# Attention in a fused trunk kernel: one score round for each query tile over three PSUM banks, the product with V placed a step later

## The chip, the cores and the metric

The kernel runs on one core of one Trainium2 chip. The metric is the device time of one execution in microseconds (us). Engines are named as in the profile: PE is TensorE, DVE is VectorE, ACT is ScalarE, POOL is GpSimd, SP issues most transfers.

## What is computed

One layer of a hybrid trunk, for a prompt of 1024 tokens and 8 sample groups of 16 tokens (1152 tokens in all, D = 1024). One input projection feeds an attention branch and a Mamba-2 branch; both are projected back, gated, merged and added to x. All of it is float32. The part that the change touches is the attention of the prompt: 16 heads of 64, chunks of 64 tokens, each chunk attends to itself and to the eight chunks before it.

```python
def attend(q, k, v, bias, mask):
    s = jnp.einsum('bqhd,bkhd->bhqk', q, k).astype(jnp.float32) * (ATT_HEAD_DIM ** -0.5) + bias[None].astype(jnp.float32)
    s = jnp.where(mask, s, -1e30)
    p = jax.nn.softmax(s, axis=-1).astype(v.dtype)
    return jnp.einsum('bhqk,bkhd->bqhd', p, v)
```

## The kernel before

**Stages.** Norm and modulation come first, then the eight units of the attention (two heads each), then dt and the 16 head pairs of the second branch, then the projections. Every stage has a `dense_gen` with the large matmuls and generators with everything else. `run` (line 732) records the program: it draws dense matmuls one after the other, adds their cost to a planned `clock`, and lets the other generators (`urgent`, `paced`) take a step whenever the planned time and their credit allow. `until(t)` and `pause(t)` hold a generator until that planned time.

**Large matmuls.** A projection weight is split into a high and a low float32r part (ACT copy at line 321, DVE subtraction at line 322), the activations too, and each product is three matmuls of 128x128 by 384 columns: lines 384, 385 and 387 (`dense`) and 438 to 440 (`dense_tok`, for q, k and v of a unit, nine token tiles of 128). They accumulate in the two banks of pool `psd`.

**A unit's attention** runs beside the dense matmuls of the next unit. `prelude` normalises q and k on POOL, transposes them (lines 857 and 867) and splits them. `prompt` (line 915) then works on query tiles m = 0 to 7 of 128 tokens; tile m sees n = min(m, 4) + 1 key tiles, so four of the eight tiles see five, 640 columns. `sample` (line 979) does the sample tokens, with matmuls of 32-column tiles (lines 1002, 1005, 1028).

For a query tile, `prompt` does this:

- scores (line 939): six matmuls for each column range, three terms for each of two heads. The head's 64 dims are the rows, so the two heads use the two row halves of the array (64x128 tiles). The result goes to the one tile of pool `pss`, two banks, one for each head. With 640 columns there are two rounds of 320, the second behind the emptying of the first
- `negated` (line 901): DVE adds the bias and takes the smallest value, one instruction for each head and round
- `exps` (lines 896 to 898): ACT's exponential with the row sum, DVE's reciprocal and scaling, into places `S` of the arena
- a step later, `transposed` (lines 903 to 913): PE transposes the probabilities of tile m-1 in groups of up to four (line 908) through a bank `g` of pool `psg` (four banks); ACT (line 910) or DVE (line 912) copies them to another place `S`
- right behind, after a planned pause, the product with V of the same tile m-1 (line 969): 2n matmuls with 64 columns each, the two heads in the two column halves (128x64 tiles), into a bank `g`; DVE multiplies with the gate z (line 974).

**What sets the order.** The recorded program is reordered for each engine by a scheduler that uses durations of its own; engines then run their queues in order, with semaphores for every dependency. `late` (line 268) pins an instruction behind what was recorded before it on its engine; later recorded work can still be moved ahead of it. In the kernel before, the scores' and V's matmuls at lines 939 and 969 are not pinned, `negated` is. `sfree` is the planned time at which the score tile is free again; `walloc` waits for a place in the arena.

Of the kernel before, what the change touches and what calls it, by code (L numbers as in the profile page):

```python
# [18 lines left out]
NT = NP + NB * NS  # L19
G3 = NT // 3  # L20
NH = 16
HD = 64
# [89 lines left out]
def trunk_kernel(ctx: ExitStack, tc: tile.TileContext, h):  # L112
    nc = tc.nc
# [3 lines left out]
    pss = ctx.enter_context(tc.tile_pool(name="pss", bufs=1, space=bass.MemoryType.PSUM))  # L117
# [3 lines left out]
    arena = Arena(base, FCOLS)  # L121
# [46 lines left out]
    for n, w in PARAMS:  # L168
# [24 lines left out]
    Z0 = fixed[0] + 2 * 1024  # L193
    XW = 3 * 288 + 2 * 256
    L_RAW = arena.set_layout(fixed[0], [("raw", 2, 1024)])
    L_ATT = arena.set_layout(Z0, [("Q", 1, 18 * P), ("T", 5, NT), ("S", 8, 640), ("U", 2, 640), ("K", 4, 512), ("q", 2, 256), ("d", 2, 256),
                                  ("p", 2, 128), ("n", 2, 36 + 3 * 16), ("t", 4, 14)])
    L_ATT["Z"] = L_ATT["T"][2:]
    L_SSD = arena.set_layout(Z0, [("X", 1, XW), ("R", 2, 1184), ("t", 8, 36), ("pad", 1, 576), ("T", 9, NT), ("Y", 1, 1184), ("H", 1, 1024),
# [68 lines left out]
    late = tc.keep_in_program_order  # L268
# [61 lines left out]
    def get_w(i):  # L330
        while w_left(i):
            w_split(i)
        return wsplit[i][:2]
# [119 lines left out]
    for k in range(KT):  # L453
        b = alloc(L_START, "T", NT)
# [73 lines left out]
    ms = {}  # L528
# [73 lines left out]
    v = [sm.ap[:, i * 9:(i + 1) * 9] for i in range(4)]  # L602
# [15 lines left out]
    x = xs_in[0]  # L618
# [13 lines left out]
    for g, tok in enumerate(groups):  # L632
        ps = pg(G3)
# [43 lines left out]
    get_w(2)  # L677
    z_first = alloc(L_ATT, "T", NT)
    d_first = alloc(L_ATT, "T", NT)

# [15 lines left out]
    clock = [0.0]  # L696
# [91 lines left out]
    sfree = [0.0]  # L788
    zs = {0: z_first}

    def attention(u):
        st = {"n": 0}
        lay = L_ATT
        big = "Z" if u == NU - 1 else "T"
# [99 lines left out]
        def exps(p, sm_, e):  # L894

            nc.scalar.activation(p, p, AF.Exp, bias=sm_[:, 4 + e:5 + e], scale=-1.0, accum_out=sm_[:, 6 + e:7 + e])  # L896
            nc.vector.reciprocal(sm_[:, 8 + e:9 + e], sm_[:, 6 + e:7 + e])
            nc.vector.tensor_scalar(p, p, sm_[:, 8 + e:9 + e], None, ALU.mult)

        def negated(p, least, ps, bap):  # L900
            late(nc.vector.tensor_tensor_reduce(p, ps, bap, -1.0, 3.0e38, ALU.add, ALU.min, least))  # L901

        def transposed(p, pt, nt):
            for j in range(0, nt, 4):
                n = min(4, nt - j)
                ps = pg()
                for s in range(n):
                    nc.tensor.transpose(ps[:, s * P:(s + 1) * P], p.ap[:, (j + s) * P:(j + s + 1) * P], ident)  # L908
                if j == 0:
                    nc.scalar.activation(pt.ap[:, j * P:(j + n) * P], ps[:, :n * P], AF.Copy)  # L910
                else:
                    nc.vector.tensor_copy(pt.ap[:, j * P:(j + n) * P], ps[:, :n * P])
            p.free()

        def prompt():
            yield from ready(lambda: "left" in st)
            yield from until(st["t"])
            qh, ql, kh, kl = st["ops"]
            v, z, bias = (st[n] for n in ("v", "z", "bias"))
            prev = None  # L920
            for m in range(9):
                n = min(m, 4) + 1
                np_ = min(m - 1, 4) + 1
                pr, pts = [], []
                if m < 8:

                    for e in range(2):
                        pr.append([(yield from walloc(lay, "S", 640)), 0])
                    sm_ = yield from walloc(lay, "t", 14)
                    cols = [(0, 320), (320, 320)] if n == 5 else [(0, n * P)]  # L930
                    qs = slice(m * P, m * P + P)
                    for a, (c, w) in enumerate(cols):
                        yield from until(sfree[0])
                        ps = pss.tile([P, 2, 512], F32, tag="s", name=nm("s"))
                        kk = slice((m + 1 - n) * P + c, (m + 1 - n) * P + c + w)
                        for i, (x, y) in enumerate(((qh, kh), (qh, kl), (ql, kh))):
                            for e in range(2):
                                hs = slice(HD * e, HD * e + HD)
                                nc.tensor.matmul(ps[:, e, :w], x.r[hs, qs], y.r[hs, kk], start=i == 0, stop=i == 2)  # L939
                        for e in range(2):  # L940
                            b = bias[e].ap[:, (5 - n) * P + c:(5 - n) * P + c + w]
                            least = sm_.ap[:, 2 * a + e:2 * a + e + 1] if n == 5 else sm_.ap[:, 4 + e:5 + e]
                            negated(pr[e][0].ap[:, c:c + w], least, ps[:, e, :w], b)
                        yield 3 * (w / 2.27 + 10)
                        sfree[0] = clock[0] + 2 * (w + 160) + 300
                    if n == 5:
                        nc.vector.tensor_tensor(sm_.ap[:, 4:6], sm_.ap[:, 0:2], sm_.ap[:, 2:4], ALU.min)
                    for e in range(2):
                        exps(pr[e][0].ap[:, :n * P], sm_.ap, e)
                        pr[e][1] = clock[0] + 3800 + 700 * e  # L950
                    sm_.free()
                if m == 7:
                    for x in st["ops"]:
                        x.free()
                    for b in bias:
                        b.free()
                if m:
                    for e in range(2):
                        pt = yield from walloc(lay, "S", 640)
                        yield from until(prev[e][1])  # L960
                        transposed(prev[e][0], pt, np_)
                        pts.append(pt)
                        yield 109 * np_
                    yield from pause(1100)
                    ps = pg(P)
                    for j in range(np_):
                        for e in range(2):
                            vc = (m - np_ + j) * P + e * HD
                            nc.tensor.matmul(ps[e * HD:e * HD + HD, :], v.ap[:, vc:vc + HD], pts[e].ap[:, j * P:(j + 1) * P],  # L969
                                             start=j == 0, stop=j == np_ - 1)  # L970
                    for x in pts:
                        x.free()
                    ms = slice((m - 1) * P, m * P)
                    nc.vector.scalar_tensor_tensor(z.ap[:, ms], ps, 0.5, z.ap[:, ms], ALU.mult, ALU.mult)
                    yield 2 * np_ * 103 + 200
                prev = pr
            done()

        def sample():
# [769 lines left out]
```

## Time and profile before

| what | value |
|---|---|
| median of 3 runs | 2037.41 us (2037.35 to 2038.08) |
| the profiled execution | 2043.03 us |
| its span, first to last instruction | 2041.2 us |
| instructions in it | 35394 |
| mean granted TensorE clock | 0.994 |
| chain of work that ended last | PE 96%, DVE 2%, DMA 1%, ACT 1% |
| scores of 320 columns, line 939 | 45.0 us (256) and 19.9 us (128, from `qa_att`) |
| product with V, line 969 | 84.3 us, 960 (two passes of each of 480) |
| transposes of probabilities, line 908 | 82.5 us, 560 |
| `negated`, line 901, DVE | 99.5 us, 208 |
| exponentials, line 896, ACT | 101.2 us, 144 |

The busy time of a group is the time that its instructions cover; matmuls overlap, so PE's groups are read by the starts of their instructions. A row of the timeline is start, duration, engine, line, form (rows*columns of the array's tile, and the moving operand) and how many were merged. A row of the stretches gives, behind the stretch and its length, the busy time of PE, weight loads (PEld), DVE, ACT and POOL, then the granted clock, the DMA share and GB/s.

### The profile page before, as it was taken

Reading aid. Unit: us, or ns where it says so; the run is one execution under the profiler, and the core shown is the slowest. Engines: PE = TensorE matmul, PEld = TensorE weight load, DVE = VectorE, ACT = ScalarE, POOL = GpSimd, SP = SyncE. Lnnn points to the kernel's source line nnn. Section 1 sums busy time; section 2 is a strip of 40 time slices with the busy share of each in tenths; the row PEclk is TensorE's granted clock in tenths of the full one; section 3 lists DMA queues with packets and bytes.
Section 4 is the critical chain, followed back from the end, with each engine's and each line's share of the span. In section 5 each row is a group of like instructions: output and inputs, shape, how many; then the busy total and the mean of one; then the engine's idle time right before and its main releaser. Section 6 shows DMA issues by size and latency. Waiting matters only on the chain.

```text
span 2041.2 us, 35394 instructions
## 1 busy us (share of the span) xinstructions
PE 2014.5 (99%) x14223; PEld 1879.7 (92%) x14223; DVE 1163.9 (57%) x2424; ACT 766.0 (38%) x1560; POOL 405.9 (20%) x657
## 2 busy tenths in 40 slices
PE   7999999999999999999999999999999999999999
PEld 5888888888888888999999999999999999999999
DVE  6445454554554566456775677557764533777732
ACT  5344443443434444444534444345443311111210
POOL 0123121231212210123332234224323210000000
PEclk9999999999999999999999999999998999999999
DMA  7233232332323232333333433243325663331331
GB/s 311 88 103 104 72 127 76 127 101 95 110 86 127 68 102 84 103 123 120 121 99 111 124 109 121 93 126 128 120 89 191 251 224 103 126 100 54 100 118 62
DMA packets 81371, 239.63 MB, mean 117 GB/s; under 512 B 14316, under 2 KB 15352, under 8 KB 81208
## 3 DMA queue, kind: packets, MB, share of 16 engines
q1 hardware_dynamic: 72248, 208.73, 31.3%
q0 software_dynamic: 8960, 28.65, 3.6%
q8 instruction: 112, 1.84, 0.4%
q14 instruction: 51, 0.42, 0.1%
HBM read 193.39 MB, written 43.95 MB: 116 GB/s over the span
## 4 chain that ended last, share of the span: by engine, by line
PE 96%; DVE 2%; DMA 1%; ACT 1%; issue 0%; SPq 0%; DVEq 0%; ACTq 0%
PE d L384 13%; PE d L387 13%; PE d L385 13%; PE s L384 5%; PE d L440 5%; PE s L385 5%; PE d L438 5%; PE s L387 5%; PE d L439 5%; PE g L969 4%; PE g L908 3%; PE s L939 3%; PE g L1385 2%; PE g L1358 1%; PE g L1405 1%; PE g L1028 1%
## 5 line engine op out<-in xcount | busy, mean ns | idle before, releaser
L384 PE MATMUL d<-rarena 128*128 128x384 f32 x1536 | 527.8, 344 | 1.0 <-ACT rarena L321 1.0
L385 PE MATMUL d<-rarena 128*128 128x384 f32 x1536 | 518.3, 337 | 0.0
L387 PE MATMUL d<-rarena 128*128 128x384 f32 x1536 | 517.5, 337 | 0.2 <-DVE rarena L322 0.2
L384 PEld LDWEIGHTS d<-rarena 128*128 128x128 f32 x1536 | 289.7, 189 | 6.3 <-issue 3.8
L387 PEld LDWEIGHTS d<-rarena 128*128 128x128 f32 x1536 | 289.4, 188 | 3.0 <-issue 2.1
L385 PEld LDWEIGHTS d<-rarena 128*128 128x128 f32 x1536 | 290.0, 189 | 1.8 <-issue 1.5
L321 ACT ACTIVATE rarena<-arena 128x1024 fp32r<-128x1024 f32 x97 | 102.6, 1058 | 301.0 <-PE s L385 188.6
L384 PE MATMUL s<-rarena 128*128 128x384 f32 x624 | 213.6, 342 | 1.3 <-DVE arena L901 1.3
L385 PE MATMUL s<-rarena 128*128 128x384 f32 x624 | 209.7, 336 | 0.0
L387 PE MATMUL s<-rarena 128*128 128x384 f32 x624 | 209.5, 336 | 0.0
L438 PE MATMUL d<-va_att,rarena 128*128 128x384 f32 x576 | 200.1, 347 | 0.3 <-DVE arena L689 0.3
L440 PE MATMUL d<-va_att,rarena 128*128 128x384 f32 x576 | 199.4, 346 | 0.0
L439 PE MATMUL d<-va_att,rarena 128*128 128x384 f32 x576 | 198.0, 344 | 0.0
L322 DVE TENSOR_TENSOR rarena<-arena,rarena 128x1024 fp32r<-128x1024 f32 x97 | 125.9, 1298 | 94.3 <-ACT rarena L321 93.3
L901 DVE CUSTOM_DVE_ANT_0 arena<-s,arena 128x320 f32<-128x320 f32 (+5 forms) x208 | 99.5, 513 | 135.1 <-PE s L939 112.3
L896 ACT ACTIVATE arena<-arena 128x640 f32<-128x640 f32 (+3 forms) x144 | 101.2, 706 | 97.0 <-DVE arena L901 51.8
L384 PEld LDWEIGHTS s<-rarena 128*128 128x128 f32 x624 | 117.8, 189 | 3.4 <-issue 1.6
L385 PEld LDWEIGHTS s<-rarena 128*128 128x128 f32 x624 | 117.9, 189 | 0.4 <-issue 0.4
L387 PEld LDWEIGHTS s<-rarena 128*128 128x128 f32 x624 | 117.6, 188 | 0.0
L440 PEld LDWEIGHTS d<-va_att,rarena 128*128 128x128 f32 x576 | 108.3, 188 | 7.0 <-issue 6.3
L438 PEld LDWEIGHTS d<-va_att,rarena 128*128 128x128 f32 x576 | 108.4, 188 | 6.8 <-issue 5.6
L910 ACT ACTIVATE arena<-g 128x512 f32<-128x512 f32 (+3 forms) x144 | 71.0, 522 | 114.0 <-PE g L908 113.6
(332 smaller groups left out, 3358.7 us busy)
## 6 DMA issues: line engine op xcount, KB each, us to landing
arena<-in_wall_dram SPq DMA_DIRECT2D x88, 512.0 KB, 3.9
arena<-in_kc_dram SPq DMA_DIRECT2D x64, 256.0 KB, 3.0
arena<-in_vc_dram SPq DMA_DIRECT2D x64, 256.0 KB, 2.8
arena<-acs_d SPq DMA_DIRECT2D x20, 576.0 KB, 3.6
gate_d<-arena POOLq DMA_DIRECT2D x48, 192.0 KB, 2.2
y_d<-arena POOLq DMA_DIRECT2D x15, 576.0 KB, 3.4
arena<-y_d SPq DMA_DIRECT2D x15, 576.0 KB
arena<-in_wssd_dram SPq DMA_DIRECT2D x16, 512.0 KB, 3.5
```

The costliest lines, as they stand in the source:

```text
L321: keep(nc.scalar.activation(hi.r[:, c], b.ap, AF.Copy))
L322: keep(nc.vector.tensor_tensor(lo.r[:, c], b.ap, hi.ap[:, c], ALU.subtract))
L384: nc.tensor.matmul(ps, hi.r[:, wc], kh.r[:, tok], start=k == 0, stop=False)
L385: nc.tensor.matmul(ps, hi.r[:, wc], kl.r[:, tok], start=False, stop=False)
L387: nc.tensor.matmul(ps, lo.r[:, wc], kh.r[:, tok], start=False, stop=k == nk - 1)
L438: nc.tensor.matmul(ps, kh.r[:, tok], hi.r[:, wc], start=k == 0, stop=False)
L439: nc.tensor.matmul(ps, kh.r[:, tok], lo.r[:, wc], start=False, stop=False)
L440: nc.tensor.matmul(ps, kl.r[:, tok], hi.r[:, wc], start=False, stop=k == KT - 1)
L896: nc.scalar.activation(p, p, AF.Exp, bias=sm_[:, 4 + e:5 + e], scale=-1.0, accum_out=sm_[:, 6 + e:7 + e])
L901: late(nc.vector.tensor_tensor_reduce(p, ps, bap, -1.0, 3.0e38, ALU.add, ALU.min, least))
L910: nc.scalar.activation(pt.ap[:, j * P:(j + n) * P], ps[:, :n * P], AF.Copy)
L969: nc.tensor.matmul(ps[e * HD:e * HD + HD, :], v.ap[:, vc:vc + HD], pts[e].ap[:, j * P:(j + 1) * P], start=j == 0, stop=j == np_ - 1)
```

## The change

The edit is in the arena's layout and in `prompt`. A tile of five key tiles gets its scores in one round: columns 0 to 319 go to the two banks of `pss`, columns 320 to 639 to two banks `g`, and the four `negated` follow together. The product with V is moved from tile m-1 to tile m-2, its matmuls are recorded directly behind the scores of tile m, and both are pinned with `late`; the loop has two more steps than tiles instead of one. The gate follows the round's `negated`. The planned times (`sfree`, `tpt`) change with it. The arena has nine places `S` instead of eight and one place `q` (squares of q and k, line 806) instead of two.

```diff
-    L_ATT = arena.set_layout(Z0, [("Q", 1, 18 * P), ("T", 5, NT), ("S", 8, 640), ("U", 2, 640), ("K", 4, 512), ("q", 2, 256), ("d", 2, 256),
+    L_ATT = arena.set_layout(Z0, [("Q", 1, 18 * P), ("T", 5, NT), ("S", 9, 640), ("U", 2, 640), ("K", 4, 512), ("q", 1, 256), ("d", 2, 256),
...
+            def weigh(j, po):
+                n = min(j, 4) + 1
+                for i in range(n):
+                    for e in range(2):
+                        vc = (j + 1 - n + i) * P + e * HD
+                        late(nc.tensor.matmul(po[e * HD:e * HD + HD, :], v.ap[:, vc:vc + HD], pts[j][e].ap[:, i * P:(i + 1) * P],
+                                              start=i == 0, stop=i == n - 1))
+                for x in pts.pop(j):
+                    x.free()
+                return 2 * n * 103 + 200
...
-            for m in range(9):
+            for m in range(10):
...
-                    cols = [(0, 320), (320, 320)] if n == 5 else [(0, n * P)]
-                    for a, (c, w) in enumerate(cols):
-                        yield from until(sfree[0])
-                        ps = pss.tile([P, 2, 512], F32, tag="s", name=nm("s"))
+                    yield from until(max(sfree[0], tpt.get(m - 2, 0.0)))
+                    ps = pss.tile([P, 2, 512], F32, tag="s", name=nm("s"))
+                    if m > 1:
+                        po = pg(P)
+                    cols = [(0, min(n * P, 512), [ps[:, e, :] for e in range(2)])]
+                    if n == 5:
+                        cols = [(0, 320, cols[0][2]), (320, 320, [pg() for _ in range(2)])]
...
-                                nc.tensor.matmul(ps[:, e, :w], x.r[hs, qs], y.r[hs, kk], start=i == 0, stop=i == 2)
+                                late(nc.tensor.matmul(pt[e][:, :w], x.r[hs, qs], y.r[hs, kk], start=i == 0, stop=i == 2))
+                        cost += 3 * (w / 2.27 + 10)
+                    if m > 1:
+                        cost += weigh(m - 2, po)
+                    for a, (c, w, pt) in enumerate(cols):
                         for e in range(2):
...
-                            negated(pr[e][0].ap[:, c:c + w], least, ps[:, e, :w], b)
-                        yield 3 * (w / 2.27 + 10)
-                        sfree[0] = clock[0] + 2 * (w + 160) + 300
+                            negated(pr[e].ap[:, c:c + w], least, pt[e][:, :w], b)
+                    yield cost
+                    sfree[0] = clock[0] + 2 * (n * P + 160) + 300
...
+                else:
+                    yield from until(tpt[m - 2])
+                    po = pg(P)
+                    yield weigh(m - 2, po)
+                if po is not None:
+                    gated(m - 2, po)
...
-                    yield from pause(1100)
-                    ps = pg(P)
-                    for j in range(np_):
-                        for e in range(2):
-                            vc = (m - np_ + j) * P + e * HD
-                            nc.tensor.matmul(ps[e * HD:e * HD + HD, :], v.ap[:, vc:vc + HD], pts[e].ap[:, j * P:(j + 1) * P],
-                                             start=j == 0, stop=j == np_ - 1)
-                    for x in pts:
-                        x.free()
-                    ms = slice((m - 1) * P, m * P)
-                    nc.vector.scalar_tensor_tensor(z.ap[:, ms], ps, 0.5, z.ap[:, ms], ALU.mult, ALU.mult)
-                    yield 2 * np_ * 103 + 200
-                prev = pr
+                    tpt[m - 1] = clock[0] + 1100
+                    sfree[0] = max(sfree[0], clock[0] + 1500)
```

More of the change, by code (lines that the diff above doesn't have):

```diff
@@ L919, in prompt, with gated @@
             v, z, bias = (st[n] for n in ("v", "z", "bias"))
-            prev = None
-            for m in range(9):
+            probs, pts, tpt = {}, {}, {}
+            def weigh(j, po):
[8 more added lines that the diff above has]
+                return 2 * n * 103 + 200
+            def gated(j, po):
+                ms = slice(j * P, (j + 1) * P)
+                nc.vector.scalar_tensor_tensor(z.ap[:, ms], po, 0.5, z.ap[:, ms], ALU.mult, ALU.mult)
+            for m in range(10):
                 n = min(m, 4) + 1
-                np_ = min(m - 1, 4) + 1
-                pr, pts = [], []
+                po = None
                 if m < 8:
+                    pr = []
                     for e in range(2):
-                        pr.append([(yield from walloc(lay, "S", 640)), 0])
+                        pr.append((yield from walloc(lay, "S", 640)))
                     sm_ = yield from walloc(lay, "t", 14)
-                    cols = [(0, 320), (320, 320)] if n == 5 else [(0, n * P)]
+                    yield from until(max(sfree[0], tpt.get(m - 2, 0.0)))
[5 more added lines that the diff above has]
+                        cols = [(0, 320, cols[0][2]), (320, 320, [pg() for _ in range(2)])]
                     qs = slice(m * P, m * P + P)
-                    for a, (c, w) in enumerate(cols):
-                        yield from until(sfree[0])
-                        ps = pss.tile([P, 2, 512], F32, tag="s", name=nm("s"))
+                    cost = 0
+                    for c, w, pt in cols:
                         kk = slice((m + 1 - n) * P + c, (m + 1 - n) * P + c + w)
@@ L948, in prompt @@
                     for e in range(2):
-                        exps(pr[e][0].ap[:, :n * P], sm_.ap, e)
-                        pr[e][1] = clock[0] + 3800 + 700 * e
+                        exps(pr[e].ap[:, :n * P], sm_.ap, e)
+                    probs[m] = pr, clock[0] + 3800
                     sm_.free()
+                else:
[4 more added lines that the diff above has]
+                    gated(m - 2, po)
                 if m == 7:
@@ L956, in prompt @@
                         b.free()
-                if m:
+                if 0 < m < 9:
+                    n = min(m - 1, 4) + 1
+                    pts[m - 1] = []
+                    pr, t0 = probs.pop(m - 1)
+                    yield from until(sfree[0])
                     for e in range(2):
                         pt = yield from walloc(lay, "S", 640)
[L960 to L963, printed above, removed]
-                    yield from pause(1100)
-                    ps = pg(P)
-                    for j in range(np_):
-                        for e in range(2):
-                            vc = (m - np_ + j) * P + e * HD
-                            nc.tensor.matmul(ps[e * HD:e * HD + HD, :], v.ap[:, vc:vc + HD], pts[e].ap[:, j * P:(j + 1) * P],
-                                             start=j == 0, stop=j == np_ - 1)
-                    for x in pts:
-                        x.free()
-                    ms = slice((m - 1) * P, m * P)
-                    nc.vector.scalar_tensor_tensor(z.ap[:, ms], ps, 0.5, z.ap[:, ms], ALU.mult, ALU.mult)
-                    yield 2 * np_ * 103 + 200
-                prev = pr
+                        yield from until(t0 + 700 * e)
+                        transposed(pr[e], pt, n)
+                        pts[m - 1].append(pt)
+                        yield 109 * n
+                    tpt[m - 1] = clock[0] + 1100
+                    sfree[0] = max(sfree[0], clock[0] + 1500)
             done()
```

## The prediction

> **What bounds the kernel now.** I read the engine line first, then a table by stretches, PE's waits, and the timeline of PE at the attention's own matmuls.
>
> ```profile
> PE 2014.5 (99%) x14223; PEld 1879.7 (92%) x14223; DVE 1163.9 (57%) x2424; ACT 766.0 (38%) x1560; POOL 405.9 (20%) x657
> ```
>
> PE is the bound. In the stretches (busy us, instructions and granted clock), the attention from 150 to 750 us and a stretch of the second branch read:
>
> ```profile
> 150.00:750.00 600.00, 598.84 (x4635) 511.94 (x4634) 306.07 (x970) 249.36 (x601) 132.59 (x263) 1.00 0.30 98
> 900.00:1050.00 150.00, 150.00 (x1073) 148.02 (x1072) 100.78 (x157) 66.96 (x134) 46.65 (x61) 1.00 0.36 117
> ```
>
> PE is busy for 99.8% of both (598.84 of 600, 150 of 150), but weight loads fill 85% (511.94 of 600) against 99%. A busy PE row therefore hides time in the attention. The Trainium skill says so ("Perfetto Trace Analysis", Identifying the Most-Contended Engine): matmul occupancy tells little of headroom, weight loads tell more. By the first column alone a change that only reorders PE could win nothing; by the second it can. The waits (total, times, longest) are few:
>
> ```profile
> PE g L1385 <- DVE arena L1438: 4.2, 1, 4.2
> ...
> PE s L384 <- DVE arena L901: 1.3, 1, 1.3
> ...
> PE s L939 <- DVE arena L901: 0.3, 1, 0.3
> ```
>
> Only the last two are behind score work, and both are in the last unit, after 800 us. So there is hardly a stall in the attention that a shorter chain could remove. What is there is the price of interruptions (start, us, line, form):
>
> ```profile
> 190.35 0.34 PE L440 MATMUL d<-va_att,rarena 128*128 128x384 f32 x1
> 190.62 0.43 PE L969 MATMUL g<-arena 128*64 128x128 f32 x2
> 190.98 0.44 PE L438 MATMUL d<-va_att,rarena 128*128 128x384 f32 x1
> 191.27 0.33 PE L439 MATMUL d<-va_att,rarena 128*128 128x384 f32 x1
> ```
>
> ```profile
> 426.01 0.34 PE L439 MATMUL d<-va_att,rarena 128*128 128x384 f32 x1
> 426.28 0.41 PE L939 MATMUL s<-rarena 64*128 64x320 f32 x2
> 426.53 0.31 PE L939 MATMUL s<-qa_att,rarena 64*128 64x320 f32 x2
> 426.68 0.31 PE L939 MATMUL s<-rarena 64*128 64x320 f32 x2
> 426.91 0.44 PE L440 MATMUL d<-va_att,rarena 128*128 128x384 f32 x1
> 427.19 0.34 PE L438 MATMUL d<-va_att,rarena 128*128 128x384 f32 x1
> ```
>
> ```profile
> 203.78 0.34 PE L387 MATMUL d<-rarena 128*128 128x384 f32 x1
> 203.96 0.60 PE L857 MATMUL g<-arena 128*128 128x128 f32 x4
> 204.31 0.42 PE L384 MATMUL d<-rarena 128*128 128x384 f32 x1
> 204.57 0.34 PE L385 MATMUL d<-rarena 128*128 128x384 f32 x1
> ```
>
> Dense matmuls start every 0.174 us. One product with V (128*64) between two of them moves 190.35 to 191.27: 0.92 - 2 x 0.174 = 0.57 us. Three pairs of scores (64*128; the second and third pair follow 0.25 and 0.15 later) take 427.19 - 426.01 - 0.348 = 0.83, where three pairs at 0.147 would be 0.44: 0.39 is the interruption. Four transposes (128*128, as the dense ones) take 0.79 - 0.348 = 0.44, that is 4 x 0.109: no charge. **So each run of matmuls in half or quarter tiles costs 0.35 to 0.39 us over its steady pace, and transposes cost nothing extra.** For a V run the parts are 0.268 - 0.174 going in, 0.160 - 0.109 in the first pair, 0.203 - 0.109 going out, and 0.281 - 0.174 in the first dense matmul: 0.346 in all.
>
> **The change part by part.** It adds or removes no matmul, DVE, ACT or POOL instruction and no DMA; only order, banks and places change. In the built orders I counted runs of scores, V and sample matmuls not broken by a dense matmul or a transpose:
>
> - Runs: 190 before, 161 after; in a steady unit 24 and 20. 29 fewer x 0.35 to 0.39 = -10.1 to -11.3 us. The scheduler still splits many rounds; only some are twelve scores and ten V matmuls in one piece. Changes of tile form inside a run are 61 and 62, so they cancel.
> - V matmuls run two at a time, in the two column halves; a group of odd length leaves one alone, which costs about 0.105 (0.210 alone, 0.109 for a pair's half of the passes). Such groups fall from 74 to 46: -2.9. Odd groups of scores rise from 8 to 18; a lone one takes a pair's step of 0.14 where half of it is its share: 0.07 each, +0.7.
> - Transposes are cut into 268 runs instead of 212, at 0.005 each: +0.3.
>
> By hand: -12.0 to -13.2. More exactly, I gave each of the 14,222 steps from one matmul's start to the next in the changed order the median of the same step (kind, width, tile, what stood ahead) in the trace; 14,101 have an exact twin. That sum is 1997.4 us for the old order and 1985.9 for the new: **-11.5**, of which 1.64 in each steady unit (86.67 to 85.03; the trace has 87.38 between units, 0.7 more, which I leave in). The old sum lacks 29.7 us of waits, half clock and spread (2027.1 from first to last start); I take them as unchanged.
>
> New waits: PE reaches scores, transposes or V behind DVE or ACT. In the trace the shortest margin at such a place between 150 and 730 us is 0.6 us. In the new order, second-half scores take two of the four `g` banks and the product a third; transposes queue behind a round's reductions, for a bank. A reduction of 320 columns follows the last each 0.42 us on DVE, the first 0.34 after the last score pair starts, so the third is done after about 1.6; transposes that wait for it stand at least 3.0 us behind in the seven steady units: margin 1.4. The `z` gate behind two 512-wide reductions is tightest, a few tenths. Cost: from 0 to 0.5 x 7 = 3.5 us; I take 0, since both bounds of the chain come out ahead of PE. A transpose or score that did wait would hold every dense matmul behind it, PE being in order.
>
> One place `q` instead of two: ACT's second square waits for DVE's reduction L809 (0.41 us) of the token tile before; tiles are 24 x 0.174 = 4.2 us apart, so it is hidden; without that cover each of 72 tiles would pay the square and the sum, 0.38 + 0.41: 57 us. The ninth place `S` and the product's lag of one tile cost no instruction. No transfer moves past another in SP's or POOL's queue by the edit itself, and the longest DMA waits of PE are at the start. The order of the last 3473 matmuls (from 1441 us on) is unchanged.
>
> The profiled execution took 2043.0 (span 2041.2 and 1.8 around it), 5.6 over the median of the runs, 2037.4. The sum gives 2031.5 for a profiled execution and 2025.9 by the median. **I predict 2026.**
>
> **The rivals.**
>
> *Half clock, so no change (0.07).* At the end of the attention:
>
> ```profile
> 808.29 0.65 PE L384 MATMUL s<-rarena 128*128 128x384 f32 x1 [1.31 <-DVE arena L901]
> 808.74 0.52 PE L385 MATMUL s<-rarena 128*128 128x384 f32 x1
> ```
>
> From here to 811.6 dense matmuls start 0.32 apart instead of 0.174, which loses 3.4 x (1 - 0.174 / 0.32) = 1.6 us. Before it lie 4.7 us with scores, transposes and a wait but no dense matmul. The longest stretch without one is 3.39 us in each new steady unit. If each led to half clock, 7 x 1.6 = 11.2 would eat the gain: 2037. Against it: the old order, by the same steps, has such stretches of 3.62 us once a unit, and the granted clock stays 1.00 there. The Trainium skill ("TensorE: Matmul & The Clock Gate", Parts 1 and 4) has half clock after about 3.4 us of idle array, and says that transposes do not count as activity; by that rule both orders are near the edge, and this trace does not show it for unit-long stretches.
>
> *A bank that comes too late: slower (0.08).* In 32 rounds (four full tiles, eight units) transposes need a `g` bank which the new round holds until its third or fourth reduction. If DVE first finishes a normalisation (0.55), a copy (0.29), a sum (0.41) and another copy (0.29), 1.54 goes against a margin of 1.4, and a further normalisation makes the wait 0.7: 32 x 0.7 = 22.4, so 2048. It decides from 11.5 / 32 = 0.36 us a round. The Trainium skill warns of this side ("TensorEngine Tiling (Array Packing)", PSUM Bottleneck): packing speeds PE but not the emptying of banks, and asks for both ScalarE and VectorE, where here DVE empties all score banks. DVE is 51% busy in the stretch, which speaks against.
>
> *More (0.06).* The 4.2 us wait at L1385, near 1536 us, follows one subtraction L322 of 4.09 us (mean 1.30) and is followed by 9.2 us at a granted clock of 0.50; together about 8.8. If the shift in time spares it: 2017.
>
> *The last unit loses more or less (inside the forecast).* Waits and half clock cost 6.8 us from 700 to 850; the new order has about as many short leads there. I allow 4 either way.
>
> **How the numbers follow.** Forecast 0.79: 2026, own range 2020 to 2032 (hand sum, gate, last unit). For 8 in 10 with part of the rivals: 2017 to 2034. About 0.2% (4 us) is what a measurement here can tell from no change: faster 0.79 + 0.06 = 0.85, same 0.07, slower 0.08.
>
> **What would show it.** Right: units 85.7 us apart (first sample score to first), PE's idle in the attention still near nothing, granted clock 1.00 from 150 to 700, weight loads at a larger share than 85%. Wrong: a repeated wait of transposes on reductions or the gate; half clock in steady units; a unit near 87 although the runs are fewer, which would mean that an interruption costs less when joined runs are longer.

## The result and the profile after

| | before | after |
|---|---|---|
| median | 2037.38 us (2035.56 to 2038.13, 6 runs) | 2021.84 us (2019.75 to 2023.59, 6 runs) |
| ratio, 95% interval | | 0.9919 [0.9909, 0.9929] |
| profiled execution, its span | 2043.03, 2041.2 | 2019.75, 2017.9 |
| first to last PE start in it | 2027.1 | 2004.5 |
| runs of scores, V and sample matmuls | 190 | 161 |
| one steady unit, first sample score to first | 87.38 | 85.50 |

The change gains 15.5 us, 0.8%. Medians below are set against the runs of before that share their chip (2037.6 to 2038.1).

Engines (first line) and chain of waits (second) on the page of the kernel after:

```profile
PE 1994.6 (99%) x14223; PEld 1869.1 (93%) x14223; DVE 1165.6 (58%) x2424; ACT 771.5 (38%) x1560; POOL 407.2 (20%) x657
...
PE 98%; DVE 1%; DMA 0%; ACT 0%; issue 0%; SPq 0%; ACTq 0%; DVEq 0%
```

PE busy fell by 19.9 us (2014.5 to 1994.6) with the same 14,223 matmuls: they did not become fewer, they stand in a better order. The stretches that the prediction read, of the kernel after:

```profile
150.00:750.00 600.00, 599.19 (x4743) 517.70 (x4743) 323.35 (x1007) 263.36 (x620) 129.32 (x258) 1.00 0.32 101
900.00:1050.00 150.00, 150.00 (x1121) 147.58 (x1117) 106.26 (x162) 69.31 (x143) 53.31 (x68) 1.00 0.37 117
```

In 150 to 750 the PE column does not move (598.84 to 599.19); the count does, 4635 to 4743 matmuls in the same 600 us, and weight loads rise from 511.94 to 517.70, 85.3% to 86.3%. That is the second column doing what the prediction asked of it. The second branch, which the change leaves alone, is still at 98%. Its count differs too (1073 and 1121), but there the same stretch of time lies some 20 us further on in the program, so it holds other work.

Some of PE's waits after (total, times, longest; L597 belongs to the first stage):

```profile
PE g L1410 <- DVE arena L1463: 4.4, 1, 4.4
PE s L597 <- DVE rarena L584: 3.4, 4, 1.6
...
PE d L384 <- ACT rarena L321: 0.4, 1, 0.4
```

The two waits behind `negated` (1.3 and 0.3) are gone; the 4.2 at L1385 is still there (L1410 after), so nothing spared it. One full round of the kernel after (scores L961, V L928, transposes L908):

```profile
421.79 0.34 PE L438 MATMUL d<-va_att,rarena 128*128 128x384 f32 x1
422.05 0.41 PE L961 MATMUL s<-rarena 64*128 64x320 f32 x2
...
422.89 0.31 PE L961 MATMUL g<-rarena 64*128 64x320 f32 x2
423.13 1.31 PE L928 MATMUL g<-arena 128*64 128x128 f32 x20
424.37 0.66 PE L908 MATMUL g<-arena 128*128 128x128 f32 x4
424.79 0.43 PE L439 MATMUL d<-va_att,rarena 128*128 128x384 f32 x1
425.05 0.34 PE L440 MATMUL d<-va_att,rarena 128*128 128x384 f32 x1
```

Read as in the prediction, up to the second dense matmul behind the run, this takes 425.05 - 421.79 = 3.26 us. The work in it is 2 x 0.174 + 6 x 0.147 + 10 x 0.109 + 4 x 0.109 = 2.76: a charge of 0.5 for scores and V together, where two runs apart would have paid 0.35 and 0.39. Joining saves about 0.24 and not a whole price, because the change of form inside the run costs too, about 0.14: the first V starts 0.24 behind the last pair of scores instead of 0.147, and the first two passes of V start 0.16 apart instead of 0.109.

The last unit, 700 to 850 us, before (first fence) and after (second):

```profile
700.00:850.00 150.00, 147.23 (x1112) 130.13 (x1111) 79.67 (x207) 66.46 (x139) 17.88 (x45) 0.98 0.31 99
```

```profile
700.00:850.00 150.00, 149.19 (x1129) 134.02 (x1128) 86.62 (x210) 69.64 (x148) 20.70 (x54) 1.00 0.29 94
```

PE idle falls from 2.77 to 0.81 us, and the two half-clock stretches of before (at 733.2 and 808.3 us, 3.4 us each) are gone: granted clock 0.98 to 1.00. The stretch at 733.2 has nothing to do with the attention's chain. It begins behind 18 small matmuls of the dt stage, recorded back to back with PE busy throughout:

```profile
731.07 2.14 PE L1114 MATMUL g<-arena,va_ssd 64*128 64x32 f32 x18
733.14 0.65 PE L384 MATMUL d<-rarena 128*128 128x384 f32 x1
```

In the kernel after, the scheduler happens to place them in two pieces, 14 and 4, with dense matmuls between:

```profile
714.58 1.74 PE L1139 MATMUL g<-arena,va_ssd 64*128 64x32 f32 x14
...
720.65 0.63 PE L1139 MATMUL g<-arena,va_ssd 64*128 64x32 f32 x4
```

**Where 15.5 went.** In the two traces the way from the first to the last PE start is 22.6 us shorter. The attention's steps, each at its median over the kernels run here, sum to 11.0 us less (10 to 13 by other ways of grouping the steps). PE's waits fall from 22.9 to 19.5 us in all, 2.0 of it in the last unit. The time at half clock before the last instructions falls from 23.9 to 6.8 us, worth about 17.1 x (1 - 0.174 / 0.32) = 7.8. Together that is 22.2.

That is more than the timed 15.5, since the profiled execution of before lies 5.6 above its median and that of after 2.1 below, and half clock differs from execution to execution: the executions of before took 2035.0 us at a granted clock of 0.999 and 2042.2 to 2043.0 at 0.994. At an equal granted clock of 0.996 they average 2038.0 (20 executions) against 2022.7 after (2 executions), still 15.3 apart. So the timed gain is made of steps and waits, 11.0 and 3.4 in the traces; half clock adds next to nothing to it, and how much of it the two profiled executions caught is luck.

### The profile page after: what moved, and what is told of

It reads as the page before. It is cut to its first block, busy times and chain, and to the rows that moved or that the text cites. A ratio compares the mean times of both kernels' runs of the same rounds, so it can differ in the third digit from the quotient of the medians.

```text
span 2017.9 us, 35308 instructions
## 1 busy us (share of the span) xinstructions
PE 1994.6 (99%) x14223; PEld 1869.1 (93%) x14223; DVE 1165.6 (58%) x2424; ACT 771.5 (38%) x1560; POOL 407.2 (20%) x657
## 4 chain that ended last, share of the span: by engine, by line
PE 98%; DVE 1%; DMA 0%; ACT 0%; issue 0%; SPq 0%; ACTq 0%; DVEq 0%
PE d L384 14%; PE d L387 13%; PE d L385 13%; PE s L384 5%; PE s L385 5%; PE s L387 5%; PE d L438 5%; PE d L439 5%; PE d L440 5%; PE g L928 3%; PE g L908 3%; PE s L961 2%; PE g L1410 2%; PE g L1383 1%; PE g L1430 1%; PE g L385 1%
## 5 line engine op out<-in xcount | busy, mean ns | idle before, releaser
L321 ACT ACTIVATE rarena<-arena 128x1024 fp32r<-128x1024 f32 x97 | 102.6, 1058 | 301.1 <-PE s L385 191.2
L438 PEld LDWEIGHTS d<-va_att,rarena 128*128 128x128 f32 x576 | 108.7, 189 | 6.9 <-issue 5.0
L439 PEld LDWEIGHTS d<-va_att,rarena 128*128 128x128 f32 x576 | 108.5, 188 | 3.8 <-issue 3.7
L440 PEld LDWEIGHTS d<-va_att,rarena 128*128 128x128 f32 x576 | 108.5, 188 | 2.6 <-issue 2.5
```

The lines of the kernel that those rows point to most:

```text
L321: keep(nc.scalar.activation(hi.r[:, c], b.ap, AF.Copy))
L438: nc.tensor.matmul(ps, kh.r[:, tok], hi.r[:, wc], start=k == 0, stop=False)
L439: nc.tensor.matmul(ps, kh.r[:, tok], lo.r[:, wc], start=False, stop=False)
L440: nc.tensor.matmul(ps, kl.r[:, tok], hi.r[:, wc], start=False, stop=k == KT - 1)
```

## The experiments

**Theory.** PE is full; the price of an interruption times the number of runs, and lone halves, set the length of a unit; where dense matmuls are few (the last unit), waits and half clock come on top. **Rivals.** The pins alone make the order; the ninth place lets the chain run freely; the interruption has no price of its own and runs only go with something else.

A summary first. "Unit" is a steady unit in the trace, from first sample score to first (for the two with uneven units the mean of the first six). "End" is from the seventh unit's first sample score to the last attention matmul. "Lone" counts the scores, of 576, that stand in the order without one of the other half beside them; "odd V" the groups of V matmuls of odd length.

| kernel | median us | ratio [95%] | runs | lone scores, odd V | unit | end |
|---|---|---|---|---|---|---|
| before | 2037.4 | 1 | 190 | 8, 74 | 87.38 | 174.0 |
| after | 2021.8 | 0.9919 [0.9909, 0.9929] | 161 | 18, 46 | 85.50 | 165.2 |
| pins only | 2047.3 | 1.0051 [1.0036, 1.0066] | 181 | 0, 114 | 88.1 | 175.2 |
| after without pins | 2022.3 | 0.9927 [0.9912, 0.9942] | 171 | 56, 38 | 84.97 | 165.8 |
| places only | 2028.8 | 0.9956 [0.9942, 0.9971] | 177 | 0, 60 | 86.3 | 170.2 |
| one round only | 2068.7 | 1.0152 [1.0135, 1.0169] | 194 | 170, 112 | 91.4 | - |
| after, two rounds | 2032.5 | 0.9972 [0.9962, 0.9981] | 175 | 2, 32 | 85.5 | 178.9 |
| after, places of before | 2075.6 | 1.0195 [1.0173, 1.0216] | 199 | 16, 44 | 92.6 | - |
| before, all pinned | 2016.5 | 0.9891 [0.9876, 0.9906] | 165 | 0, 8 | 84.1 | 172.0 |
| after, two rounds, all pinned | 2020.1 | 0.9909 [0.9893, 0.9926] | 142 | 2, 6 | 84.6 | 175.0 |
| after, all pinned | 2000.2 | 0.9820 [0.9806, 0.9835] | 106 | 4, 6 | 82.40 | 168.1 |
| the same, longer pauses | 2005.0 | 0.9842 [0.9827, 0.9856] | 110 | 0, 4 | 82.6 | 170.3 |

### The price itself

```diff
+                if k in HALVED and tail[0]:
+                    w0 = (k * outs + o) * P
+                    for e in range(2):
+                        late(nc.tensor.matmul(ps[64 * e:64 * e + 64, :], hi.ap[:, w0 + 64 * e:w0 + 64 * e + 64], kl.ap[:, tok], start=False, stop=False))
+                else:
+                    nc.tensor.matmul(ps, hi.r[:, wc], kl.r[:, tok], start=False, stop=False)
```

The twin has one whole float32 matmul in place of the two halves; `HALVED = (2,)`, and `tail` is true for the stages behind the attention.

> The changed kernel, with 144 of the large matmuls of the stages behind the attention (one of the three terms of one row block of each) computed from float32 operands instead of float32r, as whole 128x128 tiles. By itself it only sets the base for its twin: each such matmul now takes two passes, so a time some 20 to 60 us above 2021.8 is expected by both theories.

> As its twin, but each of the 144 matmuls is cut into two of 128x64 in the two column halves of the array, which can run side by side as the products with V do. Price of an interruption (theory): each place is one run of half tiles, alone between dense matmuls, so the time stands 144 x 0.35 = 50 us above the twin (43 to 57). If the price were none, and the time of the kernels came from something else that goes with the runs: within 5 us of the twin. If the halves did not run side by side, each place would add two passes more, and the trace would show twice the steps inside the run.

Measured: 2089.48 for the twin (2 runs) and 2145.99 for the halves (2 runs): 56.5 us apart, and 56.5 / 144 = **0.39 us each**. One place in the halves, then one in the twin:

```profile
1703.18 0.34 PE L387 MATMUL s<-rarena 128*128 128x384 f32 x1
1703.45 0.87 PE L391 MATMUL s<-rarena 128*64 128x384 f32 x4
1704.25 0.45 PE L395 MATMUL s<-rarena 128*128 128x384 f32 x1
1704.53 0.34 PE L387 MATMUL s<-rarena 128*128 128x384 f32 x1
```

```profile
1700.77 0.33 PE L387 MATMUL d<-rarena 128*128 128x384 f32 x1
1700.94 0.81 PE L389 MATMUL d<-rarena 128*128 128x384 f32 x2
1701.29 0.63 PE L393 MATMUL d<-rarena 128*128 128x384 f32 x1
1701.76 0.34 PE L387 MATMUL d<-rarena 128*128 128x384 f32 x1
```

1.35 against 0.99 us for the same product, with the partners' starts 7 ns apart. Without two dense matmuls at 0.174 the twin's place takes 0.64 us, which is its two float32 passes: they start 0.32 apart. So the twin carries no charge, and the halves take 1.00, 0.36 more; the run costs 0.27 going in instead of 0.17, and the first dense matmul behind it 0.28. Over 144 places that is some 51 of the 56.5; the other 5 I have not broken down. The price agrees with the 0.35 to 0.39 read from the trace of before. The rival "no price" falls: it expected at most 5 us.

The twin itself stands 67.6 us above the kernel after, more than the 20 to 60 that I gave: 0.47 for each place, which is 2 x 0.32 for the float32 passes less the 0.174 of the float32r pass that they replace. The Trainium skill ("TensorEngine Tiling (Array Packing)", Key Properties) says that a change of tiling mode drains TensorE, without a figure; here are figures for its price, though no run shows the drain itself.

### The pins

Added to before (the first fence), taken from after (the second):

```diff
-                                nc.tensor.matmul(ps[:, e, :w], x.r[hs, qs], y.r[hs, kk], start=i == 0, stop=i == 2)
+                                late(nc.tensor.matmul(ps[:, e, :w], x.r[hs, qs], y.r[hs, kk], start=i == 0, stop=i == 2))
...
-                            nc.tensor.matmul(ps[e * HD:e * HD + HD, :], v.ap[:, vc:vc + HD], pts[e].ap[:, j * P:(j + 1) * P],
+                            late(nc.tensor.matmul(ps[e * HD:e * HD + HD, :], v.ap[:, vc:vc + HD], pts[e].ap[:, j * P:(j + 1) * P],
```

```diff
-                                late(nc.tensor.matmul(pt[e][:, :w], x.r[hs, qs], y.r[hs, kk], start=i == 0, stop=i == 2))
+                                nc.tensor.matmul(pt[e][:, :w], x.r[hs, qs], y.r[hs, kk], start=i == 0, stop=i == 2)
```

(and the same for V in `weigh`.)

> The kernel before with late on the score matmuls and on the product with V, nothing else. Price theory (time follows how often half-tile matmuls break PE's stream): 181 runs for 190, but 114 odd groups of V for 74; the sum of steps gives -0.9, so 2036 to 2037. Rival 'the pins are the gain': 2022 to 2027. Rival 'the shorter chain of one round': 2037.

> The changed kernel without late on scores and V. Price theory: 171 runs, 38 odd groups of V; sum of steps -10.5 against before, with what the last unit gave up in the changed kernel 2022 to 2027. Rival 'the pins are the gain': back to 2035 or more. Rival 'chain': 2022.

Pins alone make the kernel slower (2047.3), and without them the change is as fast as with them (2022.3 against 2021.8). "The pins make the gain" falls twice. My own number for the first, 2036 to 2037, missed by 10. I had counted 181 runs against 190 and groups of V of odd length risen from 74 to 114, since an unpinned dense matmul may still be moved between two pinned ones; but a unit is 0.7 us longer than before, and the last unit waits (PE idle 4.9 us in the end stretch, 2.8 before).

### One round, and the places, each taken by itself

```diff
-    L_ATT = arena.set_layout(Z0, [("Q", 1, 18 * P), ("T", 5, NT), ("S", 8, 640), ("U", 2, 640), ("K", 4, 512), ("q", 2, 256), ("d", 2, 256),
+    L_ATT = arena.set_layout(Z0, [("Q", 1, 18 * P), ("T", 5, NT), ("S", 9, 640), ("U", 2, 640), ("K", 4, 512), ("q", 1, 256), ("d", 2, 256),
```

> The kernel before with nine places S and one place q, nothing else. Price theory: the scheduler's order changes by itself, 177 runs for 190 and 60 odd groups for 74; sum of steps -2.8, so 2033 to 2036. Rival 'the ninth place is the gain': 2022 to 2027. Rival 'chain': 2037.

Measured 2028.8: more than half of the change's gain, from a line that adds and removes no instruction. The wait that it lifts is, by the source, one of the recording: `walloc` hands out a place earlier, and the pieces of the chain come elsewhere in the written order. The scheduler leaves 177 runs instead of 190. I had expected 2033 to 2036.

The same line undone in the kernel after:

> The changed kernel with eight places S and two places q, as before. Price theory: 199 runs, though only 44 odd groups of V; steps of 86.1 us for a unit against 85.5 in the change, and many short leads, so waits: 2028 to 2045. Rival 'the ninth place is of no use': 2020 to 2024.

Measured 2075.6, far outside what I gave. V of tile m-2 keeps a pair of probability tiles a step longer; with eight places the chain stalls in the recording and then comes at the end of each unit, with few dense matmuls between its parts. PE's waits between 150 and 850 us:

```profile
PE s L961 <- DVE arena L901: 6.6, 6, 1.1
PE g L908 <- DVE arena L897: 3.0, 6, 0.5
PE d L384 <- ACT arena L1091: 2.6, 1, 2.6
```

and the same kernel from 150 to 650 us:

```profile
150.00:650.00 500.00, 490.00 (x3657) 405.01 (x3656) 238.65 (x762) 199.09 (x473) 108.36 (x210) 0.99 0.31 99
```

PE is idle for 10 us of 500, which neither before nor after show (500.00), and the trace has six half-clock stretches in the attention. These are real stalls: the kernel has the waits of which the rivals in the prediction spoke, and the ninth place is what keeps the change free of them. They are not the whole loss: a unit is 7.1 us longer than after, and the idle time is about 1.9 of that. The order is also more broken (199 runs against 161); the rest I have not taken apart.

One round with V left at m-1 and eight places:

```diff
+                    ps0 = pss.tile([P, 2, 512], F32, tag="s", name=nm("s"))
+                    pts_ = [[ps0[:, e, :] for e in range(2)]]
+                    if n == 5:
+                        pts_.append([pg() for _ in range(2)])
...
-                                nc.tensor.matmul(ps[:, e, :w], x.r[hs, qs], y.r[hs, kk], start=i == 0, stop=i == 2)
+                                nc.tensor.matmul(pq[e][:, :w], x.r[hs, qs], y.r[hs, kk], start=i == 0, stop=i == 2)
```

> The kernel before with one score round over the two score banks and two banks g; the product with V stays with tile m-1, no pins, eight places. Price theory: 194 runs and 112 odd groups of V, because the scheduler now breaks scores and V more often; about 88.0 us between units against 87.4, so 2037 to 2046. Rival 'one round shortens the chain and that is the gain': 2022 to 2030.

Measured 2068.7, far above the 2037 to 2046 that I gave. There is no repeated wait (PE is busy 500.00 of 500 in 150 to 650). What happened stands in the timeline:

```profile
509.08 0.30 PE L944 MATMUL s<-rarena 64*128 64x320 f32 x2
509.22 0.30 PE L944 MATMUL g<-rarena 64*128 64x320 f32 x1
509.37 0.31 PE L944 MATMUL g<-qa_att,rarena 64*128 64x320 f32 x1
509.52 0.30 PE L944 MATMUL g<-rarena 64*128 64x320 f32 x1
...
511.27 0.41 PE L944 MATMUL g<-rarena 64*128 64x320 f32 x1
```

The last column is the clue: x1 where a pair says x2. The two heads' second halves write two separate banks, nothing ties them together, and the scheduler runs one head at 509 and the other at 511. 170 of 576 scores have no partner. From each score's start to the next matmul's start, all scores together take 81.4 us instead of 62.9 in the kernel before, 18.5 of the 25.7 that the trace is longer. So one round by itself, in a free order, loses.

### Two rounds in the kernel after

The kernel after, with the loop over column ranges as before and V of tile m-2 behind the second range.

```diff
-                    cols = [(0, min(n * P, 512), [ps[:, e, :] for e in range(2)])]
-                    if n == 5:
-                        cols = [(0, 320, cols[0][2]), (320, 320, [pg() for _ in range(2)])]
+                    cols = [(0, 320), (320, 320)] if n == 5 else [(0, n * P)]
...
+                    for a, (c, w) in enumerate(cols):
+                        final = a == len(cols) - 1
+                        yield from until(max(sfree[0], tpt.get(m - 2, 0.0) if final else 0.0))
```

> The changed kernel with two score rounds of 320 over the two banks again; V of tile m-2 stands behind the second round. Price theory: 175 runs, 32 odd groups of V; sum of steps -11.9, so 2021 to 2026, no worse than the change. Rival 'one round is the gain (shorter chain)': 2034 to 2038.

Measured 2032.5, slower than I gave. Units are as long as after (85.5), all of the loss of 10.7 against after lies in the end: 178.9 against 165.2. Its waits between 650 and 850 us:

```profile
PE d L384 <- ACT arena L1088: 2.9, 1, 2.9
PE d L384 <- ACT rarena L321: 2.0, 2, 1.1
PE s L1024 <- DVE arena L901: 0.5, 1, 0.5
```

with half clock at 720.1 us for 6.8. In the free order, then, two rounds lose only where dense matmuls are few. I took this for the second trip through DVE in each tile's chain, but that is not shown: the long waits are for ACT, which empties a bank of the dense matmuls (L1088) and splits weights (L321), 4.9 us together, and only 0.5 is behind `negated`. The 2.9 ends a stretch of 16.6 us, from 704.4 to 721.0, into which the scheduler put no dense matmul at all, and the half clock begins in it.

### The order as written

In all of these a scheduler reshuffles the whole unit at each edit. So the next kernels pin whatever of the attention and its dense matmuls on PE was not pinned yet, until only the last unit's attention is left:

```diff
+    def pin(x):
+        return late(x) if att_left[0] > PINTO else x
...
-                nc.tensor.matmul(ps, hi.r[:, wc], kh.r[:, tok], start=k == 0, stop=False)
+                pin(nc.tensor.matmul(ps, hi.r[:, wc], kh.r[:, tok], start=k == 0, stop=False))
```

(`PINTO = 2`; `att_left` counts the prompt and the sample part of each unit. `pin` stands around the other matmuls and transposes in the same way.)

> The changed kernel with every matmul and transpose of PE pinned while more than two attention generators are open, so that PE keeps the recorded order: 106 runs for 161, 6 odd groups of V for 46. Price theory: 83.4 us of steps for a unit against 85.4, and -16 us in all; short leads add up to 1 us of waits a unit: 2006 to 2015. Rival 'the gain was in waits, and the scheduler's freedom hides them': slower than the change, 2025 or more.

Measured 2000.2: 1.8% under before, 1.1% under after, and better than I gave. From 150 to 650 us:

```profile
150.00:650.00 500.00, 499.16 (x4152) 445.07 (x4153) 269.49 (x875) 230.38 (x541) 115.09 (x221) 1.00 0.34 108
```

4152 matmuls where after has 3974 and before 3890 in the same stretch, and weight loads at 89%. Longer planned pauses on top of it:

```diff
-                yield from pause(1300)
+                yield from pause(1800)
...
-                    tpt[m - 1] = clock[0] + 1100
-                    sfree[0] = max(sfree[0], clock[0] + 1500)
+                    tpt[m - 1] = clock[0] + 2100
+                    sfree[0] = max(sfree[0], clock[0] + 2200)
```

> As e7_all_pinned, with longer planned pauses (scores 0.7 us later, V 1.0, sample steps 1.0), which gives most leads more room, but leaves two places in each unit where PE waits over 1 us. Price theory: 83.6 us of steps for a unit, 2 to 3 us of waits: 2010 to 2022. If waits are what matters, this differs from e7 by them alone.

Measured 2005.0, below the 2010 to 2022 that I gave: the 2 to 3 us of waits in each unit did not come (PE is busy 499.99 of 500 in 150 to 650). But there was no wait to cure either, since the kernel with the shorter pauses idles 0.84 us in those 500, and there are four more runs.

With the order held, the parts can be told apart. The kernel before with all its matmuls pinned, and the two-round version pinned:

> The kernel before (two score rounds, V of tile m-1, eight places) with all matmuls and transposes pinned as in the fully pinned kernel. 165 runs against its 106, nearly no odd V group (8); sum of steps 18 us above the fully pinned kernel's, unit 85.9 against 83.3. Price theory: 2018 to 2025 if no waits come with it (the product stands a planned pause of 1.1 us behind its transposes), and below 2037.4 in any case but waits. Rival, that all of the pinned kernel's gain is the pinning and nothing the change's structure: about 2000. If waits take over: above 2037, with PE waits repeated unit by unit.

> The fully pinned kernel (2000.2) with two score rounds of 320 columns, V of tile m-2 behind the second. Now the order is as written and only this part differs: 142 runs against 106, unit by sum of steps 84.5 against 83.3. Price theory: +36 x 0.22 to 0.37 = 8 to 13 us over the pinned kernel, units about 1.2 longer; 2008 to 2013. If the last unit loses by thin cover as the two-round version of the unpinned order did (+10): up to 2023. Rival, that the one round only matters in the last unit: units as long as the pinned kernel's 82.4.

Measured 2016.5 and 2020.1. Holding the order is worth 21.7 to the kernel before by itself (2038.13 to 2016.45). The change's structure then takes off another 14 to 16 (to 2000.2: 16.2 by the medians, 14.5 by the ratios, since the two ran on different chips), nearly what it did in the free order (15.5). From before to two rounds, both pinned, V moves behind the second round and the ninth place comes with it: worth nothing (+3.7, though runs fall from 165 to 142). Joining the rounds is then worth 18 to 20 (2020.1 to 2000.2): about 13 in six units of 2.18, the rest in the end. No run has the ninth place alone, or one round with V at m-1, in the held order, so how far the two ideas need each other stays open.

The price accounts for the second step. A steady unit has 17 runs with two rounds and 12 with one: 5 x 0.35 to 0.39 is 1.75 to 1.95. One more change of form inside a run (8 against 7) takes back 0.14. The two-round kernel also waits for DVE again and again, at the second round of scores, with 3.0 us in six units, 0.5 in each. Together that is 2.1 to 2.3, measured 2.18. PE's list of waits shows them in part:

```profile
PE s L963 <- DVE arena L905: 1.8, 8, 0.2
```

It accounts for the first step only in part. Three runs fewer in a unit (17 against 20) would save 1.05 to 1.17; three more changes inside runs (7 against 4) take back 0.42, and the waits 0.5. That leaves a small gain where a unit is 0.42 longer; some 0.6 a unit stays open. The theory "one round pays only in the end", formed from the free order, falls with these two.

## Why the prediction was right, step by step

The forecast was 2026.0, the time 2021.84, inside the range and on the right side.

- **The price of interruptions: right.** 0.35 to 0.39 was read from places of the trace; 144 places made for the purpose cost 0.39 each, 0.36 in the steps at the place shown.
- **The sum of steps, -11.5: right.** With steps measured over all kernels it is -11.0 (10 to 13 by other groupings). Units were forecast at 85.7 and are 85.50: 4 runs fewer at 0.37, 3.5 lone V fewer at 0.105 and 1.25 lone scores more at 0.07 make about 1.8, and a unit is 1.88 shorter; weight loads rose by one point of share, as was to be seen.
- **New waits, taken as 0: right.** No wait of PE between 150 and 700 us behind `negated`, the gate or a bank shows in the trace:

```profile
150.00:700.00 550.00, 550.00 (x4414) 474.77 (x4415) 293.05 (x937) 242.86 (x572) 118.32 (x225) 1.00 0.33 104
```

A delay of a tenth or so would not show here, because a dense matmul's row lasts 0.33 us and the next starts after 0.174.

- **Waits, taken as unchanged: the term that was mis-sized.** "The new order has about as many short leads there. I allow 4 either way." PE's waits in the last unit fell by 2.0, of which 1.6 stood behind `negated` (1.3 and 0.3), and by 3.4 over the whole execution; the timed gain is 4.0 over the sum. A full tile makes one trip through DVE, not two, and the two waits for that trip are gone. The half clock that also went from the last unit explains no part of the timed gain: at an equal granted clock the gain is nearly the same, 15.3, and one of the two stretches had come behind dt's matmuls. That the kernel after has none there is more than the chance of one execution: the two kernels of the price experiment, whose attention is that of the kernel after, have none in their last units either, with the same end of 165.2.
- **Half clock in the steady units: did not come.** A stretch of 3.39 us without a dense matmul stands in each, at a granted clock of 1.00. The length of such a stretch alone does not decide in these traces: half clock came behind 4.7 us in before (808.3), but not behind 4.7 with the places alone (793.3) or with before pinned (777.5); behind four of the six stretches of 12 to 13.5 us in the kernel with eight places; and behind 2.9 us with dt's matmuls in it (733.2).
- **The bank that comes too late: did not come** here; but the same family of waits came in the kernel with eight places, 10 us of idle PE in 500. That kernel differs from the kernel after by the places alone; the length of DVE's queue was not varied. (The scores of a full tile use four banks, two of `pss` and two `g`, not the three of the title; with the product's, three of the four `g` banks are taken.)
- **The wait at L1385: stayed** (4.2 to 4.4).
- **What I had not asked:** how much the result rests on the scheduler's order. "Cost no instruction", said of the ninth place, is true, and still the line with the places is worth 9.2 us alone and decides whether the change works at all.

My expectations for the single parts were worse than the prediction. They were sums of steps over a built order as well. They missed where waits came (places of before, pins only, two rounds), where scores lost their partners (one round only), and where a float32 pass took longer than I thought (the twin). For the orders held as written the sum of a unit was 1.0 too high with the change (83.4 against 82.40) and 1.7 for before (85.9 against 84.16), so that before with all pinned came out just under its range (2016.5 against 2018 to 2025). The two-round pinned kernel fell into the part of its range that I had kept for the end, but it was mostly the units, which were 2.18 longer and not 1.2.

## What to carry to other kernels

Where PE reads 99% busy, count its changes of form: the order of the same matmuls was worth 37 us of 2037 here, first by joining half-tile work into longer runs and then by holding the written order against a scheduler. Do not judge the parts of a change by undoing them one at a time while a scheduler reorders everything; hold the order first, then compare. And where the dense work runs out, count the waits too: a sum of steps does not hold them, and here they were 2 of the 4 us that the forecast missed.

## What the hardware showed that I had not expected

- A float32 pass takes PE much longer than a float32r one of the same size: 384 columns start 0.32 us apart against 0.174. The 144 whole-tile float32 products of the twin cost 67.6 us, 0.47 each, which is 2 x 0.32 - 0.174. In the rows the delay shows late: the starts behind the first pass are 0.32, 0.03 and 0.47 us apart, so the float32r matmul behind it seems to start at once and the one after it pays.
- Apart from the stretch that the end of the kernel cuts off, half clock lasts 3.4, 6.8 or 10.2 us in every trace here, whole multiples. The stretches at full clock between them are whole multiples of 3.413 us too (206, 21, 212 and 145 in before). The same wait of 4.2 to 4.4 us (L1385, L1410) is followed by 10.2 in one kernel and 3.4 in another. That fits the Trainium skill ("TensorE: Matmul & The Clock Gate", Part 1): an activity window of about 3.4 us that runs on its own, so that where a gap lies in it decides what the gap costs.
- Half clock can come with PE's row full. In the 3.4 us ahead of the half clock at 733.2 in the kernel before, PE is busy 3.40 us, but with three dense matmuls, transposes, a few scores and 18 matmuls of 32 columns that take 2.1 us.
